# A trunk kernel's Strassen stage: token halves that hold half of the decode tokens, q and k in blocks of 256 weight columns, and accumulators of two PSUM banks

## The chip, the cores and the metric

One Trainium2 chip, one of its cores. The metric is the device time of one execution in microseconds (us). The kernel before takes 2266.96 us, the median of three runs (2264.1 to 2268.81).

## What is computed

One layer of a causal decoder trunk on 1024 prompt tokens and 32 decode tokens (8 sequences of 4, called the sample below). Cut to what the change touches:

```
h = rmsnorm(x, norm_w)                                  # x: 1024 (prompt) or 32 (sample) tokens x 1024
pool_in, pool_z, qk_pre, v, o_pre, m_z, if_pre, gate_pre = split(h @ w_in)
qk = silu(causal_conv4(qk_pre, conv_hist, conv_w) + conv_b)      # q, k: 4 heads x 512 columns each
hc = mlstm(heads(q), heads(k), heads(v), gates) * sigmoid(o_pre) # 4 heads x 512
bm = (head_rmsnorm(hc) * silu(m_z)) @ w_mlstm_down
```

The pooling branch, the gates, the output projection and the final norm follow. All inputs are fp32.

## The kernel before

The first stage, from about 22 to 916 us of the profile, computes q, k, v, o and z of the four heads from h and w_in. Later stages (the mLSTM, the pooling branch, the projections) are touched by the change in layout only.

**Blocks and products.** The stage is a list of 20 blocks, one for each head and each of q, v, k, o, z; a block is 512 columns of w_in against all tokens. A block is computed in the manner of Strassen: the 1024 rows of w_in, the 512 columns and the 1024 prompt tokens are each halved, and seven half-size products, named after their token operands B11, B21, M1, M2, T3, N4, B22 (`OPS`), take the place of eight. Each operand is split into a high and a low part, so each of a product's terms is three matmuls (hi by hi, hi by lo, lo by hi). A product's result is two PSUM banks of 128 partitions by 512 floats.

**The chain.** Four products accumulate in the same two banks, `self.chain`: B11, then M2, T3 and N4 on top of it. Three of the four outputs need an intermediate state of this sum, so after B11, M2 and T3 the method `save` copies both banks to SBUF with ScalarE (L97; saves a, b and c). The next product of the chain can only start on a bank when that copy has been made. `run` (L99) has the order of the products.

```python
    def save(self, name):
        tr = self.tr
        self.saved[name] = [tr.t(tr.gp, [P, 512], "s", bufs=tr.nsb) for _ in range(2)]
        for s, x in zip(self.saved[name], self.chain):
            tr.nc.scalar.activation(s, x, AF.Copy)
```

**Two kinds of block.** In q and k blocks (`ConvBlock`) weights are stationary and 512 tokens move: 24 matmuls of 512 columns a product. In v, o and z blocks (`TokBlock`) 128 tokens are stationary and 256 weight columns move: 48 matmuls of 256 columns. Both go through `half_product` (L587; the matmul is L603). The two banks are single tiles named "mm", of which there are six (`psum("psA", 6, 2)`; two more banks, "misc", serve transposes and the sample).

**Weights.** `raw_w` loads 512 rows by 256 columns as a tile "wraw"; `prep` (L75) forms sums and differences on VectorE (L80 to L86), and `split_w` makes the high part on ScalarE (L286) and the low part on VectorE (L292), 128x1024 each, one pair for each product. Each of "whi" and "wlo" has three buffers.

**The sample.** Its 32 tokens are left out of the seven products. Each block calls `few_part` (L624): 16 matmuls of 256 columns (L630), with h of the sample stationary in four groups of 32 columns. ConvBlock's `sample` (L190) copies the result to SBUF (L200), turns and adds the four groups by eight small matmuls with a selection matrix (L205), and transposes the convolution's history by four more (L203).

**After a product.** `bring` adds a saved state to a PSUM bank on VectorE, or copies the bank on ScalarE; in ConvBlock `give` (L224) then does the four-tap convolution (ScalarE L240, VectorE L242) and the SiLU (L247), and stores the result.

**The order.** `steps` (L606) issues the weight preparation of a product two or three products ahead of `run`; each engine takes its instructions in program order apart from what the scheduler interleaves. `norm_in` (L445) opens the stage: it loads, normalises and transposes the first 512 tokens, runs the first two products (`first`), then does the sample and the last 512 tokens, whose tiles borrow four "wraw" buffers (loads on L516, squares on L473), and writes the operands M1, T3, M2, N4.

Of the kernel before, what the change touches and what calls it, by code (L numbers as in the profile page):

```python
# [11 lines left out]
F32R = mybir.dt.float32r  # L12
# [6 lines left out]
P = 128  # L19
# [28 lines left out]
HT = T // 2  # L48


class Block:
# [8 lines left out]
    def __init__(self, tr, h, kind):  # L60
        self.tr, self.h, self.kind = tr, h, kind
        self.c0 = {"q": O_Q, "k": O_K, "v": O_V, "o": O_O, "z": O_Z}[kind] + h * DH
        self.tok = kind in "voz"
        self.w = [None] * 7
        self.saved = {}
        self.begin()
# [3 lines left out]

    def load(self, f):
        raw = self.tr.raw_w(self.tr.I["w_in"], self.c0, f)
        self.raw = [[r] for r in raw] if f == 0 else [a + [r] for a, r in zip(self.raw, raw)]
# [15 lines left out]
    def product(self, banks, i, start, stop):  # L89
        self.tr.half_product(banks, self.w[i], self.tr.ops[OPS[i]], self.tok, start, stop)  # L90
        self.w[i] = None
# [7 lines left out]
    def run(self, i):  # L99
        tr = self.tr  # L100
        two = lambda: [tr.mmps(), tr.mmps()]
        if i == 0:
            self.chain = two()
            self.product(self.chain, 0, True, False)
            self.save("a")
        elif i == 1:
            x = two()
            self.product(x, 1, True, True)
            for j in range(2):
                self.take(0, 0, j, x[j], self.saved["a"][j])  # L110
        elif i == 2:
            self.d = two()
            self.product(self.d, 2, True, False)
        elif i == 3:
            self.product(self.chain, 3, False, False)
            self.save("b")
        elif i == 4:
            self.product(self.chain, 4, False, False)
            self.save("c")
            self.late = [self.bring(1, 1, j, self.d[j], self.saved["c"][j]) for j in range(2)]  # L120
        elif i == 5:
            self.product(self.chain, 5, False, True)
            for j in range(2):
                self.take(1, 0, j, self.chain[j], None)
            for j in range(2):
                self.give(1, 1, j, self.late[j])
        else:
            self.product(self.d, 6, False, True)
            for j in range(2):
                self.take(0, 1, j, self.d[j], self.saved["b"][j])  # L130
            self.done()

    def take(self, fh, th, j, bank, other):
        self.give(fh, th, j, self.bring(fh, th, j, bank, other))

    def done(self):
        pass


OPS = ("B11", "B21", "M1", "M2", "T3", "N4", "B22")  # L140


class TokBlock(Block):


    def begin(self):
        tr = self.tr
        self.func = {"v": AF.Copy, "o": AF.Sigmoid, "z": AF.Silu}[self.kind]
        self.dst = {"v": tr.vD, "o": tr.oD, "z": tr.zD}[self.kind][self.h]
# [14 lines left out]
    def bring(self, fh, th, j, bank, other):  # L164
        tr, nc = self.tr, self.tr.nc
        st = tr.t(tr.gp, [P, 3 + HT + 56], "z", bufs=tr.nz)[:, :512]
        if other is None:
            nc.scalar.activation(st, bank, self.func)
        else:
            nc.vector.tensor_tensor(out=st, in0=bank, in1=other, op=ALU.add)  # L170
            if self.kind != "v":
                nc.scalar.activation(st, st, self.func)
        return st

    def give(self, fh, th, j, st):
        r0 = th * HT + j * 2 * P
        self.tr.nc.sync.dma_start(self.dst[r0:r0 + 2 * P, fh * 256:(fh + 1) * 256].rearrange("(a p) n -> p a n", p=P),
                                  st.rearrange("p (a n) -> p a n", a=2))


class ConvBlock(Block):


    def begin(self):
        self.isq = self.kind == "q"
        self.f0 = (0 if self.isq else 16) + self.h * 4
        self.cols = slice(self.f0 * P, (self.f0 + 4) * P)
        self.last = {}

    def sample(self):  # L190

        tr, nc, g = self.tr, self.tr.nc, self.tr.gp
        v = lambda x: x.rearrange("p f (b t) -> p f b t", t=7)
        self.new = tr.t(g, [P, 4, 27], "new", bufs=2)
        self.zs = tr.t(g, [P, 4, 56], "zs", bufs=2)
        h1 = tr.t(g, [P, 512], "part", bufs=2)[:24]
        nc.sync.dma_start(h1, tr.I["state_conv"][:, :, self.cols].rearrange("b j f -> (b j) f"))
        fp = tr.few_part(self.raw)
        part = tr.t(g, [P, 512], "part", bufs=2)
        nc.scalar.activation(part, fp, AF.Copy)  # L200
        ps = tr.miscps()
        for f in range(4):
            nc.tensor.transpose(ps[:, f * 24:(f + 1) * 24], h1[:, f * P:(f + 1) * P], tr.ident[:24, :24])  # L203
        for f in range(4):
            nc.tensor.matmul(ps[:, 128 + f * NS:128 + (f + 1) * NS], lhsT=part[:, f * P:(f + 1) * P], rhs=tr.sel,  # L205
                             start=True, stop=True)
        zs = v(self.zs)
        for f in range(4):
            nc.scalar.activation(zs[:, f, :, 0:3], ps[:, f * 24:(f + 1) * 24].rearrange("p (b t) -> p b t", t=3), AF.Copy)
            nc.scalar.activation(zs[:, f, :, 3:7],  # L210
                                 ps[:, 128 + f * NS:128 + (f + 1) * NS].rearrange("p (b t) -> p b t", t=DS), AF.Copy)
        for f in range(4):
            nc.gpsimd.tensor_copy(self.new[:, f, 3:27].rearrange("p (b t) -> p b t", t=3), zs[:, f, :, 4:7])

    def bring(self, fh, th, j, bank, other):
        tr, nc = self.tr, self.tr.nc
        z = tr.t(tr.gp, [P, 3 + HT + 56], "z", bufs=tr.nz)
        if other is None:
            nc.scalar.activation(z[:, 3:3 + HT], bank, AF.Copy)
        else:  # L220
            nc.vector.tensor_tensor(out=z[:, 3:3 + HT], in0=bank, in1=other, op=ALU.add)
        return z

    def give(self, fh, th, j, z):  # L224
        tr, nc, g = self.tr, self.tr.nc, self.tr.gp
        f = fh * 2 + j
        ft = self.f0 + f
        wc = lambda i: tr.cw[:, i, ft:ft + 1]
        if th == 0:
            nc.gpsimd.memset(z[:, 0:3], 0.0)  # L230
            tot = HT
            self.last[f] = tr.t(g, [P, 3], "zc", bufs=6)
            nc.gpsimd.tensor_copy(self.last[f], z[:, HT:HT + 3])
        else:
            nc.gpsimd.tensor_copy(z[:, 0:3], self.last[f])
            tot = HT + 56
            nc.gpsimd.tensor_copy(z[:, 3 + HT:], self.zs[:, f])
            nc.gpsimd.tensor_copy(self.new[:, f, 0:3], z[:, HT:HT + 3])
        acc = tr.t(g, [P, 3 + HT + 56], "z", bufs=tr.nz)[:, 3:]
        nc.scalar.activation(acc[:, :tot], z[:, 3:3 + tot], AF.Identity, scale=wc(3), bias=tr.cb[:, ft:ft + 1])  # L240
        for o in range(3):
            nc.vector.scalar_tensor_tensor(out=acc[:, :tot], in0=z[:, o:o + tot], scalar=wc(o), in1=acc[:, :tot],  # L242
                                           op0=ALU.mult, op1=ALU.add)
        if th:
            dst = (tr.qs if self.isq else tr.ks)[:, self.h * 4 + f, :].rearrange("p (b t) -> p b t", t=DS)
            nc.scalar.activation(dst, acc[:, HT:].rearrange("p (b t) -> p b t", t=7)[:, :, 3:7], AF.Silu)
        nc.scalar.activation(acc[:, :HT], acc[:, :HT], AF.Silu)  # L247
        nc.sync.dma_start(tr.qkD[self.h][:, (0 if self.isq else 4) + f, th * HT:(th + 1) * HT], acc[:, :HT])

    def done(self):  # L250
        tr, nc, O = self.tr, self.tr.nc, self.tr.O
        ps = tr.miscps()
        for f in range(4):
            nc.tensor.transpose(ps[:27, f * P:(f + 1) * P], self.new[:, f, :], tr.ident)
        st = tr.t(tr.gp, [P, 512], "part", bufs=2)[:27]
        nc.scalar.activation(st, ps[:27, :], AF.Copy)  # L256
# [4 lines left out]
class Trunk:  # L261
# [16 lines left out]
    def mmps(self):  # L278
        return self.t(self.ps, [P, 512], "mm", bufs=self.nmm)

# [72 lines left out]
    def fm(self, w, f, mov, consume, chunks=range(3)):  # L353

        kt = len(w)
        for j in chunks:
            ps = self.mmps()
            for k in range(kt):
                wh, wl = w[k][:2]
                mh, ml = mov[k]  # L360
                s = slice(j * CW, (j + 1) * CW)
# [1190 lines left out]
```

## Time and profile before

| | |
|---|---|
| median of three runs | 2266.96 us |
| the profiled execution | 2266.63 us, of which its span 2264.9 us |
| granted TensorE clock, mean of the span | 0.982 |
| TensorE busy | 2186.8 us (97%) |
| VectorE busy | 1247.0 us (55%) |
| ScalarE busy | 899.9 us (40%) |

The profile is one execution on the hardware. "Busy" of TensorE (PE) is time in which at least one matmul is in flight; its matmuls overlap, so the cost of one in a dense run is the distance from its start to the next one's start, and not its own duration. A row of the timeline has a start, a duration, the engine, the line, the operation and in brackets the idle time before it with what ended it. DVE is VectorE, ACT ScalarE, POOL GpSimd, SP the engine that issues DMAs.

### The profile page before, as it was taken

The page shows a single profiled execution, that of the slowest core. Times are in us where ns is not written, and L with a number is a line of the kernel's source. Part 1 is how long each engine was busy: PE and PEld are TensorE (multiplying, and loading weights), DVE is VectorE, ACT ScalarE, POOL GpSimd, SP SyncE. Part 2 cuts the span into 40 slices and gives each one's busy share as a digit, 9 for nine tenths or more (in the row PEclk, how much of TensorE's full clock was granted, in tenths as well). Part 3 has the DMA queues.
Part 4 walks back from the last instruction along what each step waited for, and adds up shares of the span by engine and source line. Part 5 has one row for each costly group of instructions (what it writes and reads, how often), then busy time and mean ns, then how long its engine had stood idle before and what let it go on. Part 6 is the DMA issues. An engine that isn't in the chain of part 4 may idle for free.

```text
span 2264.9 us, 37166 instructions
## 1 busy us (share of the span) xinstructions
PE 2186.8 (97%) x15071; PEld 1993.7 (88%) x15071; DVE 1247.0 (55%) x2063; ACT 899.9 (40%) x1635; POOL 145.7 (6%) x319
## 2 busy tenths in 40 slices
PE   5999999999999999999999999999998999999998
PEld 4789888988898989999999888878778999999998
DVE  7846464656554665446555675565573344543545
ACT  5535443644453444453333343222223341213443
POOL 2101010001000110000000000000000000000000
PEclk7999999999999999999999999999999999999999
DMA  4233232333243322384555454767775433323112
GB/s 142 90 110 101 83 114 87 103 100 111 70 129 95 101 75 74 106 282 152 189 167 182 153 180 154 274 241 256 265 259 201 149 117 111 105 92 118 52 48 82
DMA packets 235868, 312.52 MB, mean 138 GB/s; under 512 B 13738, under 2 KB 168986, under 8 KB 235696
## 3 DMA queue, kind: packets, MB, share of 16 engines
q1 hardware_dynamic: 235696, 310.15, 41.9%
q8 instruction: 118, 1.93, 0.4%
q14 instruction: 54, 0.44, 0.1%
HBM read 200.01 MB, written 110.45 MB: 137 GB/s over the span
## 4 chain that ended last, share of the span: by engine, by line
PE 87%; DMA 6%; DVE 3%; ACT 2%; issue 1%; SPq 1%; POOL 0%; DVEq 0%; POOLq 0%; ACTq 0%
PE mm L603 35%; PE mm L299 12%; PE mm L301 11%; PE mm L300 11%; PE misc L630 2%; PE misc L841 2%; PE num L1056 2%; PE num L299 1%; PE num L300 1%; PE num L301 1%; DMA ct<-state_mlstm_C 1%; PE kv L299 1%; PE kv L300 1%; PE kv L301 1%; DMA new_C_sample<-ct 1%; PE kv L1060 1%
## 5 line engine op out<-in xcount | busy, mean ns | idle before, releaser
L292 DVE TENSOR_TENSOR wlo<-wraw,whi 128x1024 fp32r<-128x1024 f32 (+1 forms) x196 | 235.3, 1201 | 284.6 <-ACT whi L286 279.4
L286 ACT ACTIVATE whi<-wraw 128x1024 fp32r<-128x1024 f32 (+1 forms) x196 | 203.7, 1039 | 240.8 <-PE mm L603 95.3
L299 PE MATMUL mm<-hh,whi 128*128 128x352 f32 x768 | 254.0, 331 | 13.4 <-ACT sz L1195 8.2
L301 PE MATMUL mm<-hh,wlo 128*128 128x352 f32 x768 | 251.8, 328 | 0.1
L300 PE MATMUL mm<-hl,whi 128*128 128x352 f32 x768 | 250.7, 327 | 0.0
L603 PE MATMUL mm<-whi,hl 128*128 128x256 f32 x768 | 217.6, 284 | 0.0
L603 PE MATMUL mm<-wlo,hh 128*128 128x256 f32 x768 | 214.8, 280 | 0.0
L603 PE MATMUL mm<-whi,hh 128*128 128x256 f32 x768 | 214.7, 281 | 0.0
L299 PEld LDWEIGHTS mm<-hh,whi 128*128 128x128 f32 x768 | 146.7, 191 | 25.2 <-ACT sz L1195 9.8
L242 DVE SCALAR_TENSOR_TENSOR z<-z,vcols,z 128x512 f32<-128x512 f32 (+1 forms) x192 | 143.9, 774 | 21.7 <-ACT z L240 14.6
L301 PEld LDWEIGHTS mm<-hh,wlo 128*128 128x128 f32 x768 | 146.6, 191 | 6.9 <-issue 5.0
L300 PEld LDWEIGHTS mm<-hl,whi 128*128 128x128 f32 x768 | 147.0, 191 | 5.7 <-issue 4.4
L603 PEld LDWEIGHTS mm<-whi,hh 128*128 128x128 f32 x768 | 145.0, 189 | 5.7 <-ACT part L256 3.3
L603 PEld LDWEIGHTS mm<-wlo,hh 128*128 128x128 f32 x768 | 144.5, 188 | 0.4
L603 PEld LDWEIGHTS mm<-whi,hl 128*128 128x128 f32 x768 | 144.4, 188 | 0.4
L1061 DVE SCALAR_TENSOR_TENSOR ct<-ct,dec,kv 128x512 f32<-128x512 f32 x128 | 92.4, 743 | 88.4 <-PE kv L1060 70.0
L97 ACT ACTIVATE s<-mm 128x512 f32<-128x512 f32 x120 | 71.3, 595 | 145.1 <-PE mm L603 144.4
L301 PE MATMUL mm<-mvhB,wlo 128*128 128x352 f32 x384 | 122.8, 321 | 0.0
L300 PE MATMUL mm<-mvlB,whi 128*128 128x352 f32 x384 | 122.7, 321 | 0.0
L299 PE MATMUL mm<-mvhB,whi 128*128 128x352 f32 x384 | 121.6, 323 | 0.0
L603 PE MATMUL mm<-hh,whi 128*128 128x512 f32 x256 | 103.1, 404 | 1.4 <-DVE n4l L498 1.3
L603 PE MATMUL mm<-hl,whi 128*128 128x512 f32 x256 | 102.8, 402 | 0.9 <-DVE hl L292 0.9
(434 smaller groups left out, 5790.5 us busy)
## 6 DMA issues: line engine op xcount, KB each, us to landing
wraw<-w_in SPq DMA_DIRECT2D x112, 512.0 KB
ct<-state_mlstm_C SPq DMA_DIRECT2D x32, 1024.0 KB
new_C_sample<-ct SPq DMA_DIRECT2D x32, 1024.0 KB
qkD<-z SPq DMA_DIRECT2D x64, 256.0 KB
qk<-qkD SPq DMA_DIRECT2D x16, 1024.0 KB
sgD<-sz SPq DMA_DIRECT2D x16, 528.0 KB
sg<-sgD SPq DMA_DIRECT2D x16, 528.0 KB
vD<-z SPq DMA_DIRECT2D x32, 256.0 KB
```

The source lines that it names most:

```text
L97: tr.nc.scalar.activation(s, x, AF.Copy)
L242: nc.vector.scalar_tensor_tensor(out=acc[:, :tot], in0=z[:, o:o + tot], scalar=wc(o), in1=acc[:, :tot], op0=ALU.mult, op1=ALU.add)
L286: self.nc.scalar.activation(out, in_, AF.Copy)
L292: self.nc.vector.tensor_tensor(out=out, in0=in_, in1=hi.bitcast(F32), op=ALU.subtract)
L299: mm(ps, lhsT=sh, rhs=mh, start=start, stop=False)
L300: mm(ps, lhsT=sh, rhs=ml, start=False, stop=False)
L301: mm(ps, lhsT=sl, rhs=mh, start=False, stop=stop)
L603: mm(out, lhsT=st[k], rhs=mv[k], start=start and opens and k == 0 and n == 0, stop=stop and k == 3 and n == 2, skip_group_check=True)
L630: self.nc.tensor.matmul(ps[g, f * 256:(f + 1) * 256], lhsT=self.hs[:, k, :], rhs=raw[k // 4][f][:, k % 4, :], start=k < 4, stop=k >= 4)
L841: nc.tensor.matmul(out, lhsT=qk[:, 4 + d, i * L:(i + 1) * L], rhs=qk[:, d, i * L:], start=d == 0, stop=d == 3)
L1056: nc.tensor.matmul(num[32 * d:32 * d + 32, 0, :], lhsT=qm[:, b * P + d * NS:b * P + (d + 1) * NS], rhs=ct[:, d, :], start=b == 0, stop=b = ...
L1061: nc.vector.scalar_tensor_tensor(out=ct[:, d, :], in0=ct[:, d, :], scalar=self.dec[:, h * DB + b, 1:2], in1=kv, op0=ALU.mult, op1=ALU.add)
```

## The change

The two token halves become 528 columns: 512 prompt tokens and 16 of the sample. So the sample's columns run inside the seven products wherever tokens move, that is in q and k.

- q and k blocks take 256 weight columns instead of 512 (`FeatBlock`, `ConvBlock` with a group g of 0 or 1): 16 blocks instead of 8. Their feature halves are 128 wide, and one product is 24 matmuls of 264 columns (L154), two for each term, since 528 floats do not fit a bank. `few_part` and the selection matmuls go for these blocks; the history's transposes stay, two a block (L277).
- One split of 128x1024 now serves two products of a q or k block.
- A product's result is one tile of two banks, "mm2", of which there are three; `save` of a FeatBlock is one ScalarE instruction over both banks (L161), that of a TokBlock two (L219). TokBlocks keep their size, their 48 matmuls (L211) and `few_part`.
- In `norm_in` the sample's norm and transposes come before the first products.
- Tiles of h and of later operands hold [512 prompt, 16 sample] twice; the pooling branch reads them in four pieces of 264 instead of three of 352, and two transposes of history a tile instead of one; the gate rows likewise.

```diff
 class Block:
+    def run(self, i):
+        tr = self.tr
+        if i == 0:
+            self.chain = tr.mm2()
+            self.product(self.chain, 0, True, False)
+            self.save("a")
...
+        elif i == 3:
+            self.product(self.chain, 3, False, False)
+            self.save("b")
+        elif i == 4:
+            self.product(self.chain, 4, False, False)
+            self.save("c")
...
+class FeatBlock(Block):
+    def prep(self, i):
+        tr, (r1, r2) = self.tr, self.r
+        tt = tr.nc.vector.tensor_tensor
+        f1, f2 = slice(0, P), slice(P, 2 * P)
+        if i == 0:
+            self.w[0] = tr.split_w(r1[:, :, f1])
+        elif i == 1:
+            hi, lo = tr.split_w(r2)
+            self.w[1], self.w[5] = [(hi[:, :, f], lo[:, :, f]) for f in (f1, f2)]
...
+    def product(self, ps, i, start, stop):
+        (wh, wl), (ah, al) = self.w[i], self.tr.ops[OPS[i]]
+        for j in range(2):
+            c = slice(j * CH, (j + 1) * CH)
+            for k in range(4):
+                for n, (st, mv) in enumerate(((wh, ah), (wh, al), (wl, ah))):
+                    self.tr.nc.tensor.matmul(ps[:, j, :CH], lhsT=st[:, k], rhs=mv[k][:, c],
+                                             start=start and k == 0 and n == 0, stop=stop and k == 3 and n == 2,
+                                             skip_group_check=True)
+
+    def save(self, name):
+        tr = self.tr
+        self.saved[name] = tr.t(tr.gp, [P, HH], "s", bufs=tr.nsb).rearrange("p (a n) -> p a n", a=2)
+        tr.nc.scalar.activation(self.saved[name], self.chain[:, :, :CH], AF.Copy)
...
 class TokBlock(Block):
...
     def save(self, name):
         tr = self.tr
-        self.saved[name] = [tr.t(tr.gp, [P, 512], "s", bufs=tr.nsb) for _ in range(2)]
-        for s, x in zip(self.saved[name], self.chain):
-            tr.nc.scalar.activation(s, x, AF.Copy)
+        self.saved[name] = [tr.t(tr.gp, [P, HH], "s", bufs=tr.nsb)[:, :512] for _ in range(2)]
+        for j, x in enumerate(self.saved[name]):
+            tr.nc.scalar.activation(x, self.chain[:, j], AF.Copy)
...
-class ConvBlock(Block):
+class ConvBlock(FeatBlock):
...
+    def mm2(self):
+        return self.t(self.ps, [P, 2, 512], "mm2", bufs=3)
...
-        _ps = psum("psA", 6, 2)
+        _ps = psum("psA", 0, 2)
```

Three places show what moves on the engines. Names are tile names with their numbers. The first is TensorE in the v block of head 0, from the last matmul of M2 to the first of N4 (t3h and n4h0 are the high parts of the operands T3 and N4). Before:

```order
L603 MATMUL mm_225_853<-whi_228_907,m2l_140_423 128x256
L630 MATMUL misc_283_1384<-wraw_251_1163,hs_56_137 32x256 [waits DMAHW2_49,Activation_49]
L603 MATMUL mm_224_852<-whi_237_992,t3h_137_420 128x256 [waits Activation_49]
...
L603 MATMUL mm_225_853<-whi_237_992,t3h_137_420 128x256 [waits Activation_49]
...
L603 MATMUL mm_224_852<-whi_241_1046,n4h0_148_452 128x256 [waits Activation_49]
...
L603 MATMUL mm_225_853<-whi_241_1046,n4h0_148_452 128x256 [waits Activation_49]
```

and after:

```order
L211 MATMUL mm2_224_1043<-whi_227_1097,m2l_132_414 128x256
L277 MATMUL misc_253_1359<-ident_50_112,part_252_1357 128x24 [waits DMAHW4_49,PE_49]
...
L277 MATMUL misc_282_1649<-ident_50_112,part_281_1647 128x24 [waits DMAHW5_49,DVE_49]
...
L211 MATMUL mm2_224_1043<-whi_235_1181,t3h_129_411 128x256 [waits Activation_49]
L211 MATMUL mm2_224_1043<-wlo_236_1182,t3h_129_411 128x256 [waits DVE_49]
...
L211 MATMUL mm2_224_1043<-whi_238_1234,n4h0_140_455 128x256 [waits Activation_49]
```

Before, each product of the chain waits for ScalarE twice, once at the first matmul of either bank; now once, at its first matmul, and between M2 and T3 stand four transposes of 24 columns.

The second place is ScalarE around saves b and c of the same block. Before:

```order
L97 ACTIVATE s_243_1098<-mm_224_852 128x512 [waits PE_49]
L97 ACTIVATE s_244_1099<-mm_225_853 128x512 [waits PE_49]
L286 ACTIVATE whi_245_1103<-wraw_221_846 128x1024
L97 ACTIVATE s_247_1155<-mm_224_852 128x512 [waits PE_49]
L97 ACTIVATE s_248_1156<-mm_225_853 128x512 [waits PE_49]
```

and after:

```order
L351 ACTIVATE whi_238_1234<-wraw_214_985 128x1024 [waits DMAHW1_49,PE_49]
L219 ACTIVATE s_240_1286<-mm2_224_1043 128x512 [waits PE_49]
L219 ACTIVATE s_241_1287<-mm2_224_1043 128x512
L351 ACTIVATE whi_242_1291<-wraw_221_1037 128x1024 [waits DVE_49,Activation_49]
...
L219 ACTIVATE s_244_1343<-mm2_224_1043 128x512 [waits PE_49]
L219 ACTIVATE s_245_1344<-mm2_224_1043 128x512
```

The second save of a pair no longer has a wait of its own: the first waits for the product's last matmul, in either bank, and the second runs behind it.

The third place is the k block of head 0. TensorE before (whi_286 and whi_290 are the weights of T3 and N4):

```order
L603 MATMUL mm_267_1296<-m2h_139_422,wlo_271_1327 128x512
L603 MATMUL mm_266_1295<-t3h_137_420,whi_286_1425 128x512 [waits Activation_49]
...
L603 MATMUL mm_267_1296<-t3h_137_420,whi_286_1425 128x512 [waits Activation_49]
...
L603 MATMUL mm_266_1295<-n4h0_148_452,whi_290_1455 128x512 [waits Activation_49]
...
L603 MATMUL mm_267_1296<-n4h0_148_452,whi_290_1455 128x512 [waits Activation_49]
```

and after, in the second of the two k blocks (mm2_329 is the next block's first product):

```order
L154 MATMUL mm2_298_1769<-m2h_131_413,wlo_297_1764 128x264
L211 MATMUL mm2_329_2041<-whi_312_1924,hh_54_135 128x256 [waits DVE_49,Activation_49]
L154 MATMUL mm2_298_1769<-t3h_129_411,whi_304_1837 128x264 [waits Activation_49]
...
L211 MATMUL mm2_329_2041<-wlo_313_1925,hh_54_135 128x256 [waits DVE_49]
...
L154 MATMUL mm2_298_1769<-n4h0_140_455,whi_289_1710 128x264 [waits Activation_49]
```

with ScalarE at the same place:

```order
L298 ACTIVATE z_309_1918<-hist_280_1646 128x4x3 [waits Pool_49]
L351 ACTIVATE whi_312_1924<-wraw_310_1920 128x1024 [waits DMAHW6_49,PE_49]
L161 ACTIVATE s_307_1890<-mm2_298_1769 128x528 [waits PE_49]
L308 ACTIVATE ks_49_111<-z_292_1745 128x16 [waits DVE_49]
L309 ACTIVATE z_292_1745<-z_292_1745 128x512
```

Between M2 and T3 one matmul of the next block stands on TensorE, and on ScalarE that block's first weights are split right ahead of save b. That split's wait for TensorE is for the last but one matmul of M2, the last reader of the buffer that it takes. Between T3 and N4 stand 26 matmuls of the next block.

## Rows read from the trace of the kernel before

**Rows 1.** The page: span, engines, and two groups of section 5.

```profile
span 2264.9 us, 37166 instructions
PE 2186.8 (97%) x15071; PEld 1993.7 (88%) x15071; DVE 1247.0 (55%) x2063; ACT 899.9 (40%) x1635; POOL 145.7 (6%) x319
L292 DVE TENSOR_TENSOR wlo<-wraw,whi 128x1024 fp32r<-128x1024 f32 (+1 forms) x196 | 235.3, 1201 | 284.6 <-ACT whi L286 279.4
L242 DVE SCALAR_TENSOR_TENSOR z<-z,vcols,z 128x512 f32<-128x512 f32 (+1 forms) x192 | 143.9, 774 | 21.7 <-ACT z L240 14.6
```

**Rows 2.** Windows of the first stage: length, busy us of PE, PEld, DVE, ACT, POOL, PEclk, DMA.

```profile
12.25:76.26 64.01, 44.83 (x200) 31.38 (x198) 55.68 (x84) 37.34 (x66) 8.49 (x14) 0.74 0.32 99
76.26:300.00 223.74, 223.74 (x1560) 196.95 (x1560) 124.51 (x142) 103.75 (x162) 19.89 (x50) 1.00 0.33 101
300.00:600.00 300.00, 300.00 (x2099) 263.60 (x2098) 172.56 (x197) 137.36 (x219) 28.49 (x70) 1.00 0.32 99
600.00:916.00 316.00, 316.00 (x2297) 283.16 (x2296) 182.18 (x213) 153.44 (x234) 26.58 (x63) 1.00 0.28 88
```

**Rows 3.** Timeline of PE, matmuls of 512 and of 256 columns.

```profile
88.11 0.40 PE L603 MATMUL mm<-n4h,whi 128*128 128x512 f32 x1
...
93.50 0.39 PE L603 MATMUL mm<-hh,wlo 128*128 128x512 f32 x1
93.73 0.28 PE L603 MATMUL mm<-wlo,hh 128*128 128x256 f32 x1
...
95.26 0.29 PE L603 MATMUL mm<-whi,hl 128*128 128x256 f32 x1
```

**Rows 4.** Timeline of PE, the sample of a q and of a k block.

```profile
37.48 1.93 PE L630 MATMUL misc<-wraw,hs 128*32 128x256 f32 x32
39.34 0.42 PE L203 MATMUL misc<-ident,part 24*128 24x24 f32 x4
...
157.14 0.98 PE L205 MATMUL misc<-sel,part 128*128 128x32 f32 x8
157.95 0.47 PE L603 MATMUL mm<-hh,wlo 128*128 128x512 f32 x1
```

**Rows 5.** Timeline of PE and ACT around a save b of the first v block.

```profile
119.30 0.28 PE L603 MATMUL mm<-whi,m2l 128*128 128x256 f32 x1
119.51 0.62 PE L630 MATMUL misc<-wraw,hs 128*32 128x256 f32 x2
119.62 0.60 ACT L97 ACTIVATE s<-mm 128x512 f32<-128x512 f32 x1 [2.28 <-PE mm L603]
120.06 0.38 PE L603 MATMUL mm<-whi,t3h 128*128 128x256 f32 x1
120.11 1.05 ACT L286 ACTIVATE whi<-wraw 128x1024 fp32r<-128x1024 f32 x1
```

**Rows 6.** Timeline of ACT and PE where PE waits for a copy by ACT.

```profile
39.73 0.58 ACT L200 ACTIVATE part<-misc 128x512 f32<-128x512 f32 x1
40.37 0.85 PE L205 MATMUL misc<-sel,part 128*128 128x32 f32 x6 [0.60 <-ACT part L200]
```

**Rows 7.** Timeline of ACT, high parts of 1024 and of 512 columns, a convolution's first tap.

```profile
43.48 1.04 ACT L286 ACTIVATE whi<-wraw 128x1024 fp32r<-128x1024 f32 x1
...
51.49 0.64 ACT L286 ACTIVATE hh<-s 128x512 fp32r<-128x512 f32 x1
...
100.48 0.85 ACT L240 ACTIVATE z<-z,vcols 128x568 f32<-128x568 f32 x1
```

**Rows 8.** Timeline of the start: the late tokens' loads and their first reader.

```profile
17.96 1.05 SPq L516 DMA_DIRECT2D wraw<-x_prompt  x2
...
38.66 0.33 SPq L516 DMA_DIRECT2D wraw<-x_prompt  x1
...
41.26 0.33 SPq L516 DMA_DIRECT2D wraw<-x_prompt  x1
...
42.42 1.06 ACT L473 ACTIVATE m2h<-wraw 128x1024 f32<-128x1024 f32 x1 [2.11 <-DMA wraw<-x_prompt]
```

**Rows 9.** Timeline of PE, the last of its waits at the start.

```profile
68.67 0.50 PE L603 MATMUL mm<-m2l,whi 128*128 128x512 f32 x1 [1.52 <-DVE m2l L292]
...
71.73 0.80 PE L603 MATMUL mm<-hl,whi 128*128 128x512 f32 x1 [0.67 <-DVE hl L292]
72.33 0.63 PE L603 MATMUL mm<-hh,wlo 128*128 128x512 f32 x1
...
76.26 0.78 PE L603 MATMUL mm<-t3h,whi 128*128 128x512 f32 x1
```

More of the change, by code (lines that the diff above doesn't have):

```diff
@@ L69, in begin, with sample @@
         pass
-    def load(self, f):
-        raw = self.tr.raw_w(self.tr.I["w_in"], self.c0, f)
-        self.raw = [[r] for r in raw] if f == 0 else [a + [r] for a, r in zip(self.raw, raw)]
+    def sample(self):
+        pass
+    def run(self, i):
[5 more added lines that the diff above has]
+        elif i == 1:
+            x = tr.mm2()
+            self.product(x, 1, True, True)
+            self.take(0, 0, x, "a")
+        elif i == 2:
+            self.d = tr.mm2()
+            self.product(self.d, 2, True, False)
+        elif i == 3:
[4 more added lines that the diff above has]
+            self.save("c")
+            late = self.bring(1, 1, self.d, "c")
+            self.late = late
+        elif i == 5:
+            self.product(self.chain, 5, False, True)
+            self.take(1, 0, self.chain, None)
+            self.give(1, 1, self.late)
+        else:
+            self.product(self.d, 6, False, True)
+            self.take(0, 1, self.d, "b")
+            self.done()
@@ new lines, with __init__, begin, load @@
+class TokBlock(Block):
+    def __init__(self, tr, h, kind):
+        self.h, self.kind = h, kind
+        super().__init__(tr, {"v": O_V, "o": O_O, "z": O_Z}[kind] + h * DH)
+    def begin(self):
+        tr = self.tr
+        self.func = {"v": AF.Copy, "o": AF.Sigmoid, "z": AF.Silu}[self.kind]
+        self.dst = {"v": tr.vD, "o": tr.oD, "z": tr.zD}[self.kind][self.h]
+    def load(self, f):
+        for a, r in zip(self.raw, self.tr.raw_w(self.tr.I["w_in"], self.c0, f)):
+            a.append(r)
@@ L93, in save @@
     def save(self, name):
         tr = self.tr
-        self.saved[name] = [tr.t(tr.gp, [P, 512], "s", bufs=tr.nsb) for _ in range(2)]
-        for s, x in zip(self.saved[name], self.chain):
-            tr.nc.scalar.activation(s, x, AF.Copy)
[L99 to L149, printed above, removed]
+        self.saved[name] = [tr.t(tr.gp, [P, HH], "s", bufs=tr.nsb)[:, :512] for _ in range(2)]
@@ L162, in sample, with bring @@
         nc.sync.dma_start({"v": tr.vSD, "o": tr.oSD, "z": tr.zSD}[self.kind][self.h], res)
-    def bring(self, fh, th, j, bank, other):
+    def bring(self, fh, th, ps, other):
         tr, nc = self.tr, self.tr.nc
[L166 to L178, printed above, removed]
-class ConvBlock(Block):
+        out = []
+        for j in range(2):
+            st = tr.t(tr.gp, [P, 3 + HH + 28], "z", bufs=tr.nz)[:, :512]
+            if other is None:
+                nc.scalar.activation(st, ps[:, j], self.func)
+            else:
+                nc.vector.tensor_tensor(out=st, in0=ps[:, j], in1=self.saved[other][j], op=ALU.add)
+                if self.kind != "v":
+                    nc.scalar.activation(st, st, self.func)
+            out.append(st)
@@ new lines, in bring, with give, __init__ @@
+        return out
+    def give(self, fh, th, out):
+        for j, st in enumerate(out):
+            r0 = th * HT + j * 2 * P
+            self.tr.nc.sync.dma_start(
+                self.dst[r0:r0 + 2 * P, fh * 256:(fh + 1) * 256].rearrange("(a p) n -> p a n", p=P),
+                st.rearrange("p (a n) -> p a n", a=2))
+class ConvBlock(FeatBlock):
+    def __init__(self, tr, h, kind, g):
+        self.h, self.isq, self.g = h, kind == "q", g
+        super().__init__(tr, (O_Q if self.isq else O_K) + h * DH + g * 256)
@@ L197, in sample @@
         nc.sync.dma_start(h1, tr.I["state_conv"][:, :, self.cols].rearrange("b j f -> (b j) f"))
[L198 to L200 removed]
         ps = tr.miscps()
[L202 removed]
+        for f in range(2):
             nc.tensor.transpose(ps[:, f * 24:(f + 1) * 24], h1[:, f * P:(f + 1) * P], tr.ident[:24, :24])
[L204 to L206 removed]
@@ L207, in sample @@
[L207 to L221, printed above, removed]
+        nc.scalar.activation(self.hist, ps[:, :48].rearrange("p (f r) -> p f r", f=2), AF.Copy)
@@ L222, in bring, with give @@
+    def bring(self, fh, th, ps, other):
+        z = self.tr.t(self.tr.gp, [P, 3 + HH + 28], "z", bufs=self.tr.nz)
+        self.out(z[:, 3:3 + HH], ps, other)
         return z
-    def give(self, fh, th, j, z):
+    def give(self, f, th, z):
         tr, nc, g = self.tr, self.tr.nc, self.tr.gp
-        f = fh * 2 + j
         ft = self.f0 + f
         wc = lambda i: tr.cw[:, i, ft:ft + 1]
+        b4 = lambda x, n: x.rearrange("p (b t) -> p b t", t=n)
+        zs, samp = b4(z[:, 3 + HH:], 7), b4(z[:, 3 + HT:3 + HH], DS)
@@ L488, in norm_in @@
             norm(i, tiles[i], P)
+        norm(8, xs, NS)
+        ps = self.miscps()
+        nc.tensor.transpose(ps[:, :8], v0, self.ident[:8, :8])
+        nc.vector.tensor_copy(self.nw, ps[:, :8])
+        early, late = slice(0, HT), slice(HH, HH + HT)
         r1, r2 = [], []
         for k in range(KT):
-            ps = turned([(x, P) for x in tiles], k)
+            if k % 2 == 0:
+                two = self.mm2()
+            ps = turned(tiles, two[:, k % 2], k)
             nw = self.nw[:, k:k + 1]
-            both(self.hh[:, k, :HT], self.hl[:, k, :HT], ps, nw)
-            r = self.t(xp, [P, HT], f"n4{'hl'[k // 4]}{k % 4}")
+            both(self.hh[:, k, early], self.hl[:, k, early], ps, nw)
+            r = self.t(xp, [P, HH], f"n4{'hl'[k // 4]}{k % 4}")[:, :HT]
             if k % 2:
@@ L525, in norm_in @@
+        both(t3[0][:, :, HT:], t3[1][:, :, HT:], sums[:, 1])
+        vtt(out=sums[:, 2], in0=sums[:, 0], in1=s22, op=ALU.subtract)
+        both(m2[0][:, :, HT:], m2[1][:, :, HT:], sums[:, 2])
+        vtt(out=sums[:, 3], in0=sums[:, 2], in1=s21, op=ALU.add)
         for k in range(4):
             nw, nw2 = self.nw[:, k:k + 1], self.nw[:, k + 4:k + 5]
-            ps = turned(xb, k)
+            two = self.mm2()
+            ps = turned(xb, two[:, 0], k)
             b12 = tt()
             nc.scalar.activation(b12, ps, AF.Identity, scale=nw)
-            ps = turned(xb, k + 4)
+            a = tt()
+            vtt(out=a, in0=b12, in1=r1[k], op=ALU.subtract)
+            both(self.hh[:, k, late], self.hl[:, k, late], a)
+            ps = turned(xb, two[:, 1], k + 4)
@@ L545, in norm_in @@
+            both(hi[:, :HT], lo[:, :HT], e)
+            both(hi[:, HT:], lo[:, HT:], sums[:, 3, k])
             n4[0].append(hi)
```

283 lines of the change are left out of this document (162 added, 121 removed).

## The prediction

> **What bounds the kernel now.** I read the page first: TensorE is busy for 97% of the span, VectorE for 55% and ScalarE for 40% [rows 1]. That is an average, and the change sits in the first stage, so the windows come next. From 76.26 us to 916 us TensorE is busy in every one of them for the whole window, at a granted clock of 1.00, that is 2.4 GHz [rows 2]: 840 us without a gap, while VectorE has 56 to 58% and ScalarE 46 to 49%. In this stretch a matmul more or less is time more or less, and any wait that the change puts on TensorE is a loss at once, because none is there now. Before 76.26 us the stage starts up: VectorE is the busy engine (55.68 of 64.01 us), TensorE waits for its operands, and the clock is 0.74. Here what counts is when TensorE stops waiting.
>
> The timeline says why TensorE never waits in the long stretch. Save b of a v block starts 0.32 us after the start of the last matmul of its bank (119.30 to 119.62), the next instruction of ScalarE starts 0.49 us behind it, and the copy lasts 0.60 us [rows 5]. While the second bank of M2 is being saved, TensorE has gone on with T3 in the first bank (120.06): the two banks are released one after the other, and a wait of either is covered by half a product, 24 matmuls of 256 columns or 12 of 512, both 2.8 us.
>
> **The sum.** It is made against the profiled execution, 2266.63 us, which lies 0.33 us under the median.
>
> *Matmuls of q and k.* Twenty-three steps from 88.11 to 93.50 give 0.2343 us for a matmul of 512 columns, and thirteen from 93.73 to 95.26 give 0.1177 us for 256 [rows 3]. On the line through these two, 264 columns take 0.1213 us. Before there are 8 blocks x 168 = 1344 matmuls of 512, after 16 x 168 = 2688 of 264: 326.1 - 314.9 = +11.2 us. This price holds if a weight load for each 264 columns stays hidden; it stays hidden today behind 256 columns, where each matmul has a load of its own.
>
> *Sample of q and k.* Eight blocks lose 16 matmuls of `few_part`, 39.34 - 37.48 = 1.86 us, and eight selection matmuls, 157.95 - 157.14 = 0.81 us [rows 4]. 8 x 2.67 = -21.4 us.
>
> *Waits of the chain.* This is the part that decides. A tile now is two banks, and by the order the first matmul of T3 and of N4 waits for a save that itself waits for the product's last matmul. The half product that covered the wait is gone; what covers it is what stands between. The trace of before shows no such wait, so I build it. TensorE restarts 0.06 us after ScalarE's copy has ended (39.73 + 0.58 = 40.31, restart at 40.37) [rows 6]. In a TokBlock two saves run: 0.32 + 0.49 + 0.60 + 0.06 = 1.47 us from the start of the last matmul to the start of the next, where 0.12 us are usual: 1.35 us lost, less what stands between, at 0.06 us for each small transpose and 0.12 us for a matmul of the next block. T3: four v blocks with four transposes (1.11 each), three z blocks with one matmul (1.23) and the last z block with nothing (1.35); the o blocks have the 16 sample matmuls there, which cover it. N4: four v, three z and one o block with nothing, three o with one matmul; the last z block is covered by its sample. That is 4.4 + 3.7 + 1.35 + 8 x 1.35 + 3 x 1.23 = 24 us in 19 places.
>
> In q and k N4 is covered by some 25 matmuls of the next block, about 3 us, and costs nothing as long as the save is no later than that. At T3 it isn't covered: one or two matmuls stand there, and ScalarE first splits the next block's weights, which waits for the last but one matmul of M2. For the first block of a pair that split is 512 wide, 0.64 us, 0.54 to the next start; for the second 1024 wide, 1.04 us, 0.94 to the next start [rows 7]. Counted from that matmul: 0.32 + 0.54 + 0.61 + 0.06 = 1.53 us against 0.485 (two to the end of M2, two between): 1.04 lost; and 0.32 + 0.94 + 0.61 + 0.06 = 1.93 against 0.36: 1.57 lost. Eight of each, +20.9 us. Together +45 us in 35 places. The bounds: 0.6 us a place, if only the copy itself shows (21 us), and 0.85 us more a place, if each save finds one instruction of the convolution [rows 7] ahead of it on ScalarE (75 us).
>
> *The start.* TensorE becomes steady at 76.26 us, with four products done and one sample: 4 x 24 x 0.2343 + 2.7 = 25.2 us of work [rows 9]. After, it has also done four products, but of half the size: 4 x 24 x 0.1213 = 11.6 us. The rest, 13.6 us, is still to do. Against this the start gets shorter. Two of the four late token tiles today are loaded at 38.66 and 41.26 us only, since their buffers are held by the first block, and ScalarE waits 2.11 us for one [rows 8]; after, all four are issued at once. And VectorE has eight operations of 128x1024 less to do (1.20 us each [rows 1]), two of 512 and a dozen small ones more: 55.7 - 6.6 = 49 us. With all its idle time (8.3 us) kept, TensorE is steady at 69.7 us, with none at 61.3. I take 68, near the first, since most of this idle time is waiting for ScalarE. So +13.6 - 8.3 = +5.3 us; the ends are -1.4 (61.3) and +13.6 (still 76.26).
>
> *The rest.* The pooling branch gets 192 matmuls more, of 264 instead of 352 columns, the same columns in sum: +0.2 us, and a few transposes: I put +1.2 for both. VectorE's 35 more additions and ScalarE's table loads lie beside TensorE's work. The moved sample work of `norm_in` is in the start's sum.
>
> +11.2 - 21.4 + 45 + 5.3 + 1.2 = +41 us: **2308 us**, slower by 1.8%. Without the waits it would be -4.
>
> **The rivals.** *1. Bank by bank.* If the first matmul of a bank in fact only found its own bank's copy to wait for, as today, the waits would fall to nothing and the time would be 2266.6 - 3.7 = 2263 us: no slower, on the other side of zero by 0.16%. It decides as soon as the mean loss over the 35 places is under 0.1 us. Against it stands the order, where the second save has no wait of its own and the first matmul of T3 stands behind it; for it only that the banks are separate memories of the same size as before. The Trainium skill, PSUM — Partial Sum Buffer, section "PSUM bank collisions raise a hardware error", says to guard by bank and quadrant; by that rule a matmul into bank 0 need not wait for a read of bank 1, and two tiles would cost nothing here. The rows agree on the hardware: TensorE writes bank 0 at 120.06 while ScalarE is reading its neighbour until 120.22 [rows 5]; it is the program's tiles that are coarser. Chance 0.07.
>
> *2. The clock.* Waits on TensorE might bring the clock down. After idle times of 1.52 us and 0.67 us within 5 us, matmuls of 512 columns last 0.63 us instead of 0.40 from 72.33 to 76.26, so the clock is at 1.2 GHz for 3.9 us: some 2 us lost [rows 9]. The second block of each pair has one wait of 1.57 us every 20 us; if eight to sixteen of these bring it down, the cost is 16 to 32 us more: about 2330. Against it: those two idle times came at the end of a start-up full of waits. The Trainium skill, TensorE: Matmul & The Clock Gate, section "A second HAM failure mode: psum-queue depth-cycling", tells of a kernel whose short idles between groups of matmuls made the clock swing; by that rule this rival would be the forecast. Chance 0.10.
>
> *3. VectorE or ScalarE becomes the bound in q and k.* A block of 256 columns is 168 x 0.1213 = 20.4 us on TensorE, and VectorE has about 18 us to do for it: 12 convolution taps of some 0.77 us, 3.5 low parts of 1.20 us, and the sums of weights and products [rows 1]. With in-order queues, a product's result may be taken late and its tile come free late; there are three tiles, and the next block's third product has only 4 us of cover. One wait of 1 us in each of 16 blocks gives 2324. Chance 0.13.
>
> **How the numbers follow.** The forecast has 0.70, the rivals 0.07, 0.10 and 0.13. The bounds of the waits are -24 and +30, those of the start -7 and +8. Both ends at once are unlikely: from 2308, -24 gives 2284, and the upper side takes in rivals 2 and 3 and nearly the whole +30: 2284 to 2336. What is left out is the first rival, and part of the second. A difference of 0.2% (4.5 us) is about what a measurement of this kernel can tell from none. Faster by more needs rival 1 and a good start: 0.03. Within 0.2%: the rest of rival 1 and a little of the forecast's lower tail, 0.06. Slower: 0.91.
>
> **What would show it.** In the first stage, idle time of TensorE before matmuls of T3 and N4 on L154 and L211, ended by ScalarE's saves (L161, L219): 35 gaps of 1.0 to 1.6 us, at T3 alone in q and k. Matmuls of 264 columns 0.121 us apart. Twelve blocks with `few_part` instead of 20. TensorE steady from 68 us on. A clock of 1.00 from there to the end of the stage. The prediction is wrong if these gaps are missing or under half this size, if others of the same sum stand before first products (rival 3), or if the matmul of 264 costs more than 0.125 us, which would be 10 us by itself.

## The result

The changed kernel takes 2281.51 us (median of 11 runs, 2276.71 to 2287.82) against 2266.96 us of the kernel before (11 runs, 2259.45 to 2274.7). The ratio is 1.0064, with a 95% interval of 1.0047 to 1.0081: slower, as forecast, but by 14.6 us instead of 41, and 2.5 us below the range. The profiled execution took 2283.02 us, 16.4 us more than that of before.

The windows of the changed kernel, in the columns of [rows 2]:

```profile
12.25:76.26 64.01, 39.42 (x211) 32.81 (x211) 53.34 (x96) 34.79 (x68) 4.88 (x10) 0.84 0.30 99
76.26:300.00 223.74, 215.05 (x1820) 209.01 (x1820) 126.01 (x151) 108.75 (x193) 17.24 (x48) 1.00 0.31 97
300.00:600.00 300.00, 287.97 (x2435) 279.71 (x2433) 173.86 (x210) 143.26 (x262) 23.96 (x70) 1.00 0.32 100
600.00:916.00 316.00, 304.72 (x2593) 295.63 (x2593) 179.18 (x212) 162.14 (x281) 26.18 (x68) 1.00 0.29 91
```

TensorE, which had no gap there before, now has 8.69 + 12.03 + 11.28 = 32.0 us of idle time from 76.26 to 916 us. The clock is 1.00 in all three windows. VectorE has no more to do than before, and ScalarE 5% more.

The groups of TensorE's matmuls by line, from 71 to 947 us, tell what ended this idle time (after the bar: idle before the group, and its releasers):

```profile
L211 PE MATMUL mm<-whi,hh 128*128 128x256 f32 x768 | 216.5, 282 | 8.2 <-ACT whi L351 8.2
L154 PE MATMUL mm<-hh,whi 128*128 128x264 f32 x487 | 139.9, 287 | 4.2 <-ACT whi L351 4.2
L211 PE MATMUL mm<-whi,t3h 128*128 128x256 f32 x192 | 55.1, 287 | 4.4 <-ACT s L219 4.4
L211 PE MATMUL mm<-whi,n4h 128*128 128x256 f32 x192 | 55.1, 287 | 12.2 <-ACT s L219 12.2
L277 PE MATMUL misc<-ident,part 24*128 24x24 f32 x28 | 4.0, 218 | 3.6 <-DMA part<-state_conv 3.5
```

They are ScalarE's saves (s) ahead of T3 and N4 in v, o and z, and ScalarE's split (whi) of the next block's weights, which in q and k stands in front of save b. The last row is of the transposes that stand ahead of T3 in the v blocks: TensorE sits idle there for their own load, beside the save. The timeline shows one place of each of the first two kinds. N4 of the first v block, ScalarE and TensorE:

```profile
134.12 0.28 PE L211 MATMUL mm<-whi,t3l 128*128 128x256 f32 x1
134.44 1.08 ACT L219 ACTIVATE s<-mm 128x512 f32<-128x512 f32 x2 [5.13 <-PE mm L211]
135.58 0.39 PE L211 MATMUL mm<-whi,n4h 128*128 128x256 f32 x1 [1.18 <-ACT s L219]
```

and T3 of the second q block of head 0:

```profile
91.39 0.29 PE L154 MATMUL mm<-m2h,wlo 128*128 128x264 f32 x1
91.59 1.06 ACT L351 ACTIVATE whi<-wraw 128x1024 fp32r<-128x1024 f32 x1 [0.46 <-PE mm L154]
92.56 0.59 ACT L161 ACTIVATE s<-mm 128x528 f32<-128x528 f32 x1
92.70 0.38 PE L211 MATMUL mm<-whi,hh 128*128 128x256 f32 x1 [1.02 <-ACT whi L351]
93.20 0.39 PE L154 MATMUL mm<-t3h,whi 128*128 128x264 f32 x1
```

In the first place the step from 134.12 to 135.58 is 1.46 us where 0.12 is usual: 1.34 us lost (forecast 1.35). The two saves follow the product's last matmul by 0.32 us, as in [rows 5]. In the second place T3 starts 1.81 us after the last matmul of M2, where 0.24 would do: 1.57 lost (forecast 1.57). The bracket gives less than the loss, since the last matmul counts as in flight for some 0.16 us of each gap.

So the waits came as forecast, and yet the total did not. What made up for them shows where the sample runs. First the changed kernel, v of head 0, then three places of the kernel before, in a v block and in the k block that follows it (one matmul of the sample counts twice in these rows: x32 are the 16 of a block):

```profile
113.44 0.28 PE L211 MATMUL mm<-whi,hl 128*128 128x256 f32 x1
113.65 1.93 PE L689 MATMUL misc<-wraw,hs 128*32 128x256 f32 x32
115.52 0.39 PE L211 MATMUL mm<-whi,hh 128*128 128x256 f32 x1
115.74 0.28 PE L211 MATMUL mm<-wlo,hh 128*128 128x256 f32 x1
```

```profile
105.03 1.49 PE L630 MATMUL misc<-wraw,hs 128*32 128x256 f32 x20
106.45 0.51 PE L254 MATMUL misc<-ident,new 128*27 128x128 f32 x3
106.89 1.06 PE L630 MATMUL misc<-wraw,hs 128*32 128x256 f32 x12
...
126.01 0.63 PE L630 MATMUL misc<-wraw,hs 128*32 128x256 f32 x4
126.57 0.38 PE L603 MATMUL mm<-whi,n4h 128*128 128x256 f32 x1
...
149.45 1.91 PE L630 MATMUL misc<-wraw,hs 128*32 128x256 f32 x26
151.29 0.42 PE L203 MATMUL misc<-ident,part 24*128 24x24 f32 x4
```

In the changed kernel the 16 matmuls stand in one piece in each of its 12 blocks that have them. Before, the scheduler had broken them up: ten and six in v and o; one, two and thirteen in k, z and the later q blocks, where the one and the two stand ahead of T3 and N4 of the block before. One of the single ones is in [rows 5]. The cost of a piece, from the start of the matmul before it to the start of the second matmul behind it, less the usual steps, is 0.74 us for one matmul, 0.75 for two, 1.23 for six, 1.58 for ten, 1.96 to 2.04 for thirteen, and 2.06 for sixteen: about 0.65 us for a piece, and 0.09 for each matmul in it, as a rough line through these. Summed over all pieces, the sample's matmuls cost 62.9 us before (50 pieces) and 24.8 after (12).

The whole ledger, from the two traces, each wait taken from start to start and, as in the forecast, with 0.06 us for a small transpose that stands in it:

| term | forecast | measured |
|---|---|---|
| matmuls of q and k, 2688 of 264 for 1344 of 512 | +11.2 | +12 |
| sample: 38.1 by its matmuls, 7 by the selection | -21.4 | -45 |
| waits of the chain | +45 | +45 |
| start | +5.3 | +8.5 |
| matmuls of v, o and z, 4032 of 256 in both kernels | 0 | -5 |
| small transposes, slower steps behind a wait | 0 | +3 |
| later stages | +1.2 | -2 |
| sum | +41 | +16 |

All rows but the last two move the end of the first stage (the start of its last matmul) from 928.8 to 947.1 us; the later stages then give 2 us back. The row of v, o and z was in nobody's sum: the same matmuls of 256 columns start 0.1191 us apart on average before and 0.1178 after. No run isolates why.

### The profile page after: what moved, and what is told of

It is laid out like the page before. It is cut to its first block, busy times and chain, and to the rows that moved or that the text cites. A ratio compares the mean times of both kernels' runs of the same rounds, so it can differ in the third digit from the quotient of the medians.

```text
span 2281.3 us, 39968 instructions
## 1 busy us (share of the span) xinstructions
PE 2162.9 (95%) x16311; PEld 2047.6 (90%) x16311; DVE 1259.2 (55%) x2168; ACT 927.3 (41%) x1796; POOL 136.1 (6%) x335
## 4 chain that ended last, share of the span: by engine, by line
PE 83%; DMA 7%; ACT 3%; DVE 3%; SPq 1%; issue 1%; POOL 0%; DVEq 0%; POOLq 0%; ACTq 0%
PE mm L211 20%; PE mm L154 14%; PE mm L364 12%; PE mm L366 11%; PE mm L365 11%; PE num L1121 2%; PE misc L906 1%; PE num L364 1%; PE num L365 1%; PE num L366 1%; DMA o<-oD 1%; PE kv L364 1%; DMA ct<-state_mlstm_C 1%; PE kv L1125 1%; PE kv L365 1%
## 5 line engine op out<-in xcount | busy, mean ns | idle before, releaser
L364 PE MATMUL mm<-hh,whi 128*128 128x352 f32 (+1 forms) x832 | 265.0, 319 | 13.4 <-ACT sz L1264 8.3
L366 PE MATMUL mm<-hh,wlo 128*128 128x352 f32 (+1 forms) x832 | 262.0, 315 | 0.0
L365 PE MATMUL mm<-hl,whi 128*128 128x352 f32 (+1 forms) x832 | 260.9, 314 | 0.0
L211 PE MATMUL mm<-whi,hh 128*128 128x256 f32 x768 | 216.5, 282 | 8.2 <-ACT whi L351 8.2
L211 PE MATMUL mm<-whi,hl 128*128 128x256 f32 x768 | 216.2, 281 | 0.0
L211 PE MATMUL mm<-wlo,hh 128*128 128x256 f32 x768 | 215.7, 281 | 0.0
L364 PEld LDWEIGHTS mm<-hh,whi 128*128 128x128 f32 x832 | 158.2, 190 | 27.4 <-ACT sz L1264 10.6
L365 PEld LDWEIGHTS mm<-hl,whi 128*128 128x128 f32 x832 | 158.7, 191 | 5.7 <-issue 4.4
L366 PEld LDWEIGHTS mm<-hh,wlo 128*128 128x128 f32 x832 | 158.2, 190 | 5.5 <-issue 4.2
L211 PEld LDWEIGHTS mm<-whi,hh 128*128 128x128 f32 x768 | 144.8, 189 | 13.2 <-ACT whi L351 9.9
L154 PE MATMUL mm<-hh,whi 128*128 128x264 f32 x512 | 148.8, 291 | 8.3 <-ACT whi L351 4.8
L305 DVE SCALAR_TENSOR_TENSOR z<-z,vcols,z 128x556 f32<-128x556 f32 x192 | 144.9, 792 | 17.6 <-ACT z L303 14.3
L154 PE MATMUL mm<-hl,whi 128*128 128x264 f32 x512 | 147.0, 287 | 1.5 <-DVE hl L359 1.2
L154 PE MATMUL mm<-hh,wlo 128*128 128x264 f32 x512 | 146.5, 286 | 0.0
L211 PEld LDWEIGHTS mm<-whi,hl 128*128 128x128 f32 x768 | 144.6, 188 | 0.0
L211 PEld LDWEIGHTS mm<-wlo,hh 128*128 128x128 f32 x768 | 144.4, 188 | 0.0
```

The lines of the kernel that those rows point to most:

```text
L154: self.tr.nc.tensor.matmul(ps[:, j, :CH], lhsT=st[:, k], rhs=mv[k][:, c], start=start and k == 0 and n == 0, stop=stop and k == 3 and n == ...
L211: self.tr.nc.tensor.matmul(ps[:, t // 2, t % 2 * 256:t % 2 * 256 + 256], lhsT=st[k][:, c], rhs=mv[:, k], start=start and t % 2 == 0 and k ...
L305: nc.vector.scalar_tensor_tensor(out=acc, in0=z[:, o:o + tot], scalar=wc(o), in1=acc, op0=ALU.mult, op1=ALU.add)
L364: mm(ps, lhsT=sh, rhs=mh, start=start, stop=False)
L365: mm(ps, lhsT=sh, rhs=ml, start=False, stop=False)
L366: mm(ps, lhsT=sl, rhs=mh, start=False, stop=stop)
```

## The experiments

The theory (A), as it was put down before these runs: the waits cost what they show, then read as about 41 us, and the sample gave back 21 us more than forecast (45 and 24 by the ledger above), since a piece has a price of its own and the change left far fewer pieces. The rival (B): the gaps don't set the time, and a part of their length is hidden or moves elsewhere.

**One-bank tiles.** Each product gets two tiles of one bank again, and with them one save, copy or addition for each bank; all else of the change stays.

```diff
     def mm2(self):
-        return self.t(self.ps, [P, 2, 512], "mm2", bufs=3)
+        return [self.mmps(), self.mmps()]
...
-        tr.nc.scalar.activation(self.saved[name], self.chain[:, :, :CH], AF.Copy)
+        for j in range(2):
+            tr.nc.scalar.activation(self.saved[name][:, j], self.chain[j][:, :CH], AF.Copy)
...
-        _ps = psum("psA", 0, 2)
+        _ps = psum("psA", 6, 2)
```

> The changed kernel with each product in two tiles of one bank instead of one tile of two, and one save for each bank. Everything else of the change stays. Theory A (the changed kernel loses about 41 us in waits of TensorE for the saves, and gains about 43 us on the sample, 21 more than forecast, because the sample's matmuls now stand together): the waits go but for some tenths of a us in q and k, and the sample breaks into three pieces again in the z blocks (4 x 1.5 us), so 2281.5 - 41 + 6 = about 2246 us, faster than both. Theory B (the gaps before T3 and N4 are not what sets the time, another engine paces the stage, and the 21 us missing from the forecast are waits that cost less than their length): the gaps move elsewhere and the time stays within 10 us of 2281.

Measured: 2242.1 us (6 runs, 2237.1 to 2248.31), 0.99 of before (0.9882 to 0.9919; before took 2265.18 us in that series). Its windows:

```profile
76.26:300.00 223.74, 223.48 (x1894) 217.95 (x1892) 137.46 (x179) 113.86 (x222) 24.38 (x58) 1.00 0.33 103
300.00:600.00 300.00, 299.48 (x2538) 292.29 (x2537) 182.41 (x238) 149.62 (x304) 31.44 (x74) 1.00 0.33 103
600.00:916.00 316.00, 311.31 (x2636) 302.27 (x2635) 184.02 (x247) 158.26 (x284) 29.68 (x65) 0.99 0.30 93
```

The gaps are gone (the 4.69 us in the last window are the end of the stage, which now falls into it, and which before and after have too). The first stage is 39 us shorter than in the changed kernel. In this, T3 of the first block comes 6.4 us earlier, at 64.6 us instead of 71.0, so the two-bank tiles had also slowed the start, which I had not seen; and the z blocks' sample, in three pieces again, takes some 6 back. Theory A holds, B falls: the gaps were real. The sample of v and o stays in one piece here, so that the two-bank tiles account for the z blocks' sample alone.

**The sample whole, in the kernel before.** One ordering edge for each block.

```diff
-        for f in range(2):
+        with self.tc.issue_after(self.last.ins):
+            for f in range(2):
...
-                        mm(out, lhsT=st[k], rhs=mv[k], start=start and opens and k == 0 and n == 0,
+                        self.last = mm(out, lhsT=st[k], rhs=mv[k], start=start and opens and k == 0 and n == 0,
```

> The kernel before, with an ordering edge alone: the sample's 16 matmuls of a block may not be issued ahead of the last matmul of that block's second product. They then stand in one piece in q, k and z and in two in v and o, where before 11 of the 20 blocks had three pieces and 8 had two. Theory A (a piece costs some 0.65 us beside its matmuls): 62.9 us of sample become 8 x 2.8 + 12 x 2.05 = 47 us, so 2267 - 16 = about 2251 us. Theory B (sixteen matmuls cost the same wherever they stand): 2267 us, no change.

Measured: 2251.63 us (2250.44 to 2256.66), 0.9943 of before (0.9928 to 0.9959). The first stage ends 16.5 us earlier (912.3 instead of 928.8), 0.4 of it by an earlier start. Not a matmul is gone: 22 pieces fewer account for it, at 0.73 us each. The price of a piece is shown by this.

**Both.** One-bank tiles, and the sample in one piece everywhere.

> Both at once: the changed kernel with one-bank tiles and with the sample's matmuls of v, o and z in one piece each. Theory A: 6 us under the kernel with one-bank tiles, about 2240 us. Theory B: no different from it.

Measured: 2248.32 us (2244.97 to 2253.77), 0.9925 (0.9907 to 0.9943): a miss, 6 us above the kernel with one-bank tiles instead of 6 below. The first stage did get 5.9 us shorter; the loss comes after 1365 us, where the state matrices of the sample are loaded. The lines view of TensorE there (1365 to 1710 us), for one-bank tiles and for this kernel:

```profile
L1124 PE MATMUL num<-ct,qm 128*32 128x512 f32 x256 | 44.2, 619 | 7.1 <-DMA ct<-state_mlstm_C 6.4 <-DVE ksum L1078 0.7
```

```profile
L1125 PE MATMUL num<-ct,qm 128*32 128x512 f32 x256 | 45.6, 638 | 10.5 <-DMA ct<-state_mlstm_C 10.5
```

TensorE waits longer for these loads, and the windows from 1200 to 1600 us, again of the one and then of the other, show a granted clock of 0.96 instead of 1.00:

```profile
1200.00:1600.00 400.00, 379.64 (x2645) 328.25 (x2643) 255.55 (x528) 135.35 (x273) 24.91 (x61) 1.00 0.67 226
```

```profile
1200.00:1600.00 400.00, 376.02 (x2576) 326.19 (x2576) 253.68 (x521) 132.15 (x267) 25.73 (x61) 0.96 0.66 222
```

This is the profiled execution, whose mean clock was 0.979. The clock is not all of the loss: the two runs of this kernel with a mean clock of 0.986 and 0.987 took 2246.55 and 2244.97 us, those of one-bank tiles at 0.986 to 0.988 between 2237.1 and 2244.85. The edge is in the first stage alone, but the scheduler lays out the whole program, and from the first attention matmul on TensorE's order differs in 1387 of 7905 rows.

**Three of the four z blocks whole.** The same with `issue_after` for the z blocks of heads 0 to 2 alone, since with the fourth left as it is the later order stays what it was; and the kernel with one-bank tiles again beside it.

> The changed kernel with one-bank tiles and with the sample's matmuls in one piece in the z blocks of heads 0 to 2 (of head 3 they stay in three pieces). Where all four were whole the first stage was 6 us shorter, as forecast, but the whole run 6 us longer: from the attention on, the scheduler had laid out TensorE's order otherwise in 1387 of 7905 rows. In this kernel that order is row for row the one of the kernel with one-bank tiles. Theory A with the layout as the cause of the loss: 3 x 1.47 = 4.4 us under the kernel with one-bank tiles, about 2238 us, and from the first attention matmul on the same length as there. If the loss came from the sample's place itself: 2246 us or more.

> The kernel with one-bank tiles once more, on the same chip as the kernel with three whole z blocks, so that 4 us between the two can be told: 2242 us, 4.4 us over the other by theory A; the same or below it otherwise.

Measured: 2237.73 us (2235.88 to 2240.36), 0.9869 of before (0.985 to 0.9889), and 2243.69 us (2239.81 to 2247.55) for one-bank tiles again. 6 us apart, 4.4 expected; from the first T3 to the end of the first stage it is 838.6 against 843.0 us, 4.4 apart. Behind the first stage the traces of these two kernels have TensorE's matmuls in the same order throughout. The stretch from the first of these state matmuls to the last of the sample's is 327 us here, 326 and 324 with one-bank tiles, 334 where all four were whole. So the layout of the later stage, with the clock that went with it, was the loss, and not the sample's place. This is the fastest version of the study, 1.3% faster than before in its own series, and 1.9% faster than the change, which was measured in another.

**The split behind the save.** In the changed kernel, ScalarE's weight splits may not overtake a save.

```diff
+            with self.tc.issue_after(self.saver.ins):
+                self.hi(hi, raw)
```

> The changed kernel (two-bank tiles) with an ordering edge alone: ScalarE may not issue a weight split ahead of a save that stands before it in the program. By the order this takes the split of the next block from in front of save b, but also takes away the matmuls of the next block that covered save c, so q and k have a wait at T3 and at N4. Theory A (a wait is 0.32 + 0.61 + 0.06 - 0.12 = 0.87 us where only the save stands between, and 1.0 to 1.6 where a split stands in front): 32 gaps of 0.87 us instead of 16 of 1.24 on average, 28 instead of 20 us, so about 2289 us. Theory B: gaps of another size or no change of the time.

Measured: 2293.55 us in one run, 4.5 us more than expected; the first stage ends at 956.9 us, 9.8 us later than in the changed kernel, and 1.8 of these come before its first T3. T3 and N4 of a k block:

```profile
161.57 0.28 PE L154 MATMUL mm<-m2h,wlo 128*128 128x264 f32 x1
161.88 0.61 ACT L161 ACTIVATE s<-mm 128x528 f32<-128x528 f32 x1 [0.67 <-PE mm L154]
162.54 0.39 PE L154 MATMUL mm<-t3h,whi 128*128 128x264 f32 x1 [0.70 <-ACT s L161]
...
166.41 0.39 PE L154 MATMUL mm<-n4h,whi 128*128 128x264 f32 x1 [0.70 <-ACT s L161]
```

From 161.57 to 162.54 is 0.97 us, 0.85 lost; over the 31 such places that the trace has in q and k the mean is 0.86, expected 0.87. The price of a wait, put together from rows of a kernel that had none, is right to 0.02 us.

## Why the prediction was wrong

**The direction and the waits were right.** The order said that a product of the chain now waits for saves that wait for its last matmul, and the rows gave each link: 0.32, 0.49, 0.60 and 0.06 us. The sum of +45 came out at 45. T3 lost 1.57 us in the second block of each q and k pair (forecast 1.57) and 1.01 in the first (1.04); N4 of v and z lost 1.33 (1.35), but for the last z block, where it lost 0.54 and nothing was forecast. Something else came in at T3 of the v blocks, where the transposes ahead of it waited for their own load, beside the save: 1.09 to 1.71 us (1.11). Without two-bank tiles the stage is 39 us shorter, though the z blocks' sample costs 6 us more, which settles that the cost is theirs.

**The step that failed is the sample's term, -21.4, which measured -45.** "Eight blocks lose 16 matmuls of `few_part`, 39.34 - 37.48 = 1.86 us" [rows 4]: this is the first q block, the only block of 20 whose sample stood in one piece. It was taken for all. Two sums were missed: q and k lose 26.2 us by the pieces they really had (12.4 and 13.8), not 14.9; and v, o and z, which I had set down as unchanged, went from 36.7 to 24.8 us, because their sample is no longer broken up. In z this came with the two-bank tiles: with one-bank tiles it is broken up again. In v and o it came with something else in the change, since with one-bank tiles it stays whole; before, the three transposes of L254 stood between the ten and the six, and after they stand elsewhere, in pairs. The selection matmuls cost 0.89 us a block, not 0.81. Both sums were to be seen: [rows 5] has a single piece in it, where matmuls start 0.21 and 0.55 us apart and 0.12 is usual, and the first fence on the order in the part on the change has the same L630 row between M2 and T3. I read it only for how it covers the wait.

**The range** had bounds for the waits and for the start, and none for the sample, since I took its price for read and not estimated. That alone put the result outside: with the sample at -21.4 the time would have been about 2305 us. The matmuls of v, o and z, whose 0.1177 us a step was read from thirteen of them, took off another 5 us that were not in the sum.

**The start** was 71.0 us instead of 68, inside its bounds; by the first experiment the two-bank tiles cost 6.4 us there.

**The rivals.** By-bank waiting (0.07) did not happen: each wait ended with the last save, at the product's first matmul. The Trainium skill, PSUM — Partial Sum Buffer, section "PSUM bank collisions raise a hardware error", says to guard by bank and quadrant, and has guarding by bank as the simple version. With tiles of one bank, guarded so, TensorE was busy for 223.48 of the 223.74 us up to 300 us, which agrees. The clock (0.10) did not fall: 1.00 in all windows from 76.26 to 916 us, with 33 gaps of 0.47 to 1.36 us in them. The swings of which the Trainium skill tells in TensorE: Matmul & The Clock Gate, section "A second HAM failure mode: psum-queue depth-cycling", are not shown by this trace. VectorE as the bound (0.13) did not come: no idle of TensorE in q and k is ended by it in steady state.

**The rest** held, apart from the row of v, o and z in the ledger: 264 columns take 0.1215 us on average between undisturbed neighbours (forecast 0.1213), 12 blocks with `few_part`, gaps at T3 alone in q and k.

## What to carry to other kernels

A wait is released by the unit in which the program tracks a tile: an accumulator of two banks that is read out between its sums should be tracked bank by bank, so that one half's matmuls cover the other half's copy; here that was worth 39 us of 2281. Where a change removes an operation, price all its instances, grouped by their neighbours, before one row is taken for them all: the same 16 matmuls cost 2.05 us in one piece and 3.5 in three. And where a scheduler lays out the program, compare its whole order, also far behind the edit, before a gain or loss is put down to the edit.

## What was not expected of the hardware

- Small matmuls with a stationary operand of 32 columns cost about 0.65 us for each piece in which they stand among matmuls of 128 columns, and 0.09 us each within a piece. What takes the 0.65 us was not tried: these matmuls differ from their neighbours in the width of the stationary operand, and also in type (fp32 tiles among tiles of fp32r in the kernel).
- Thirty-three idle gaps of 0.47 to 1.36 us within 840 us left the granted clock at 1.00. In the kernel with both edits a later stage with somewhat longer waits for loads ran at 0.96.
- The stretch with the loads of the sample's state differed by 7 to 10 us (334 against 327 to 324) between two orders of the same loads and the same matmuls; in the profiled execution the slower order also had the lower clock.
